# Half of an MLP's first quarter turned from row-block products into seven block products

## The chip, the core and the metric

The kernel runs on one core of a Trainium2 chip. Its time is the device time of one execution, in microseconds; of several runs the median counts. The core has five engines with queues of their own: PE (TensorE, matmuls; PEld are its weight loads), DVE (VectorE), ACT (ScalarE), POOL (GpSimd, here mostly issuing transfers that add to what is in SBUF) and SP (issuing plain transfers). An engine starts its instructions in the order of its queue.

## The reference, cut to what matters

A two-layer encoder over 512 tokens of width 1024: attention and an MLP, then a recurrent block and an MLP, then a norm. The change is in the second MLP.

```python
def squared_relu_mlp(h, w1, w2):
    u = jax.nn.relu(h @ w1)          # 1024 -> 4096
    return (u * u) @ w2              # 4096 -> 1024
...
    h = rms_norm(x, norm_mlp[layer])
    x = x + squared_relu_mlp(h, mlp_w1[layer], mlp_w2[layer])
```

## The kernel before, in words

**Arithmetic.** Every fp32 product is made of three matmuls: both operands are split into a rounded high part (by ACT, a CAST or a scaled ACTIVATE) and a low part, operand minus high (by DVE), and high x high, high x low and low x high are added in PSUM. A weight tile so costs ACT one 1024-wide cast (`wh`) and DVE one 1024-wide subtraction (`wl`). The norm's factor per token is left out of x (only its gain g goes in: `xgh`, `xgl`) and multiplied into the MLP's result (`rr`).

**x.** x lies transposed, as eight tiles of 128 features x 512 tokens. `residual` (L767) adds the output projection to each tile and makes `xgh` and `xgl`. `Squares` adds up the squares of x over the tiles; four small matmuls (L172) sum them over the features.

**The MLP.** The 4096 hidden features are taken in four quarters; each has an upward product (x to hidden) and a downward one (hidden to the result). A quarter is two halves p = 0, 1 of 512 hidden features.

The downward products of all quarters and the upward products of the quarters 1 to 3 are done by the Strassen-Winograd scheme: the operands are cut into 2 x 2 blocks, and seven block products, P1 to P7 (`PRODUCTS`), replace eight. Blocks of weights are added with each other before (`added`: P5's and P6's sums on DVE, P7's and P4's by adding transfers that POOL issues), and so are blocks of x (`sums_of_x`, four additions on DVE for each of four pairs k of x tiles: tile k and tile 4 + k) with high and low parts of their own (`halves_of_sums`: `s41`, `s2`, `s3` and the `low` tiles). A block product is 24 matmuls of 256 columns (`up`, L991). Products add up in PSUM banks named X, V and W: P1, P6, P7 and P4 go to X, P5 and P3 to V, P2 to W, and between products what stands in a bank is copied to or combined with the slots u[0] to u[3] of the half (`leave`, L1249): `keep` says which results ACT copies out, the table behind it which DVE adds to a slot. Each slot then gets relu and square (ACT), and a high and a low part.

The first quarter is different. Its upward product is made row block by row block: eight chunks of 128 hidden features, each 24 matmuls of 512 columns (`squared`, L863; `quarters`, L1356). The first two run side by side (`beside`), since the last x tile comes late. Each chunk's result gets relu and square on ACT; two chunks make a pair for which DVE forms sums (`split`, `sums`). Beside the chunks 1 to 4, `between` (L1658) turns x, with 32 transposes on PE and eight copies on ACT, into the tiles c in which the result is collected. The sums of x for the pairs 0 and 1 are made behind chunks 4 and 5, those for pairs 2 and 3 during the first downward quarter, at set places (`leave`, places 19 to 26), since the block products need them only for the second quarter.

**What sets the order.** PE's order is the program's. In the MLP, ACT and DVE run through `Ordered`, which makes each instruction be issued behind the one written before it. `run` walks a list of steps; for step i it loads what is due at its place, handles what step i - 1 left (`leave`), prepares the weights of a later step (`prepare`, `make`: high and low part, about four steps ahead) and issues step i's matmuls. P1 comes first in a half, then P5, P6, P3, P7, P2, P4 (`UP`).

Of the kernel before, what the change touches and what calls it, by code (L numbers as in the profile page):

```python
# [64 lines left out]
def hybrid_encoder(  # L65
# [41 lines left out]
    def f(ap):  # L107
        return ap.bitcast(F32)
# [107 lines left out]

    def slab(src, cut=1, ks=range(C), at=0):
        raws = rawpools[next(loads) % len(rawpools)]
        raw = raws.tile([P, C, P], F32, tag="raw", name="raw", bufs=3 if raws is wpool else 1)
        k = slice(ks.start, ks.stop)  # L220
        nc.sync.dma_start(out=raw[:, k, :], in_=src[:, k, :])
        pool = wpools[next(slabs) % len(wpools)]
        wh = half_slab(pool, "wh", at)
        wl = half_slab(pool, "wl", at)
        for i in range(cut):
            k = slice(ks.start + i * len(ks) // cut, ks.start + (i + 1) * len(ks) // cut)
            A.copy(wh[:, k, :], raw[:, k, :])  # L227
            with tc.issue_after(behind[0]) if behind[0] else nullcontext():
                V.tensor_tensor(wl[:, k, :], raw[:, k, :], f(wh[:, k, :]), ALU.subtract)  # L229
        return wh, wl  # L230
# [535 lines left out]

    def residual(srcs, gname, begun={}, ready={}):  # L767

        for c in range(C):
            add_x(c, begun[c][0] if c in begun else dense(srcs[c], bh, bl, halves=ready.get(c)))  # L770
            halves(gname, c, x[c])

    residual(w_so, "mlp0", so, so_next)


# [23 lines left out]
    class Mlp:  # L799
# [27 lines left out]

        def __init__(self, ctx, layer):
            self.layer, self.sq, self.first = layer, Squares(), None
# [33 lines left out]
        def squared(self, c):  # L863

            if self.first is None:

                self.first = [bank("z") if self.layer else self.bank() for _ in range(2)]
                self.turns = count(2)
                ws = [slab(w_m1[self.layer, i]) for i in range(2)]
                beside(ws, xgh, xgl, self.first, {})  # L870
            if self.first:
                ps = self.first.pop(0)
            else:
                ps = dense(w_m1[self.layer, c], xgh, xgl, ps=self.bank())
            p, i, a = c // 4, c % 4 // 2, c % 2
# [95 lines left out]
        def replace(self):  # L971

            for i, t in enumerate(self.s3):
                self.A.copy(xgh[:, 2 * i : 2 * i + 2, HS:], f(t).rearrange("p (k n) -> p k n", k=2))

        def slots_of(self, p):

# [54 lines left out]
        def from_up(self, q4):  # L1032
            return self.units(
                [
                    lambda tag, p=p: w_up[self.layer, q4 - 1, p, *self.SOURCES[tag]].rearrange(
                        "p k n -> p (k n)"
# [104 lines left out]
        OPEN_AT = 36  # L1141
        UP = "P1", "P5", "P6", "P3", "P7", "P2", "P4"
        STEPS = 28

        def run(self, first, between, end):
# [4 lines left out]

            steps = []
            for q4 in range(NQ):
# [4 lines left out]
            units, ws, sums, us = {("down", 0): first}, {}, {}, {}  # L1157

            def place(i):

                return (i + self.STEPS // 2) % self.STEPS

# [57 lines left out]
            def load(i):  # L1220
                q4, at = steps[i][1], place(i)

                if i == 0:
                    self.turns = count(2)
                elif at == 0:
# [16 lines left out]
            def prepare_or_hold(i, then=None):  # L1242

                if i + 1 < len(steps) and steps[i + 1][0] == "up" and steps[i + 1][3] == "P1":
                    held.append(i + 4)
# [3 lines left out]
            def leave(i):  # L1249
# [5 lines left out]
                if kind == "down":  # L1255
                    ahead = q4 == 0 and place(i) == 25
                    if ahead:
# [4 lines left out]
                    if not ahead:  # L1262
                        prepare_or_hold(i)
                    if q4 == 0:

# [55 lines left out]
            waiting, later, held = [], [], []  # L1321
            make(0)
            add(1)
            make(1)
            add(5, 4)
            for e in (self.V, self.A):
                e.turn(True)
            self.squared(C - 1)
            self.split(1, 1, slice(0, 3), slice(0, 3))
            make(2)  # L1330
            self.sums(1, 1)
            add(4, 2)
            make(3)
            self.split(1, 1, slice(0, 4), slice(3, 7))
            between(C - 1)
            for i, (kind, q4, g, name) in enumerate(steps):
# [7 lines left out]
                if name == "P1":  # L1344
                    us[g] = self.slots_of(g)
# [6 lines left out]
            for e in (self.V, self.A):  # L1352
                e.turn(False)
            end([ws[len(steps) - 2 + g] for g in range(2)], sums["down", NQ - 1, 0]["X"])

        def quarters(self, between, end):  # L1356
# [292 lines left out]

    residual(w_ro, "mlp1", begun, {4: ws["o4"]})  # L1650
    wctx.close()


    with ExitStack() as mctx:
        lp = mctx.enter_context(tc.tile_pool(name="last", bufs=1))
        mlp = Mlp(mctx, 1)

        def between(c):  # L1658

            t = c - 1  # L1660
            if t not in range(NB):
                return
            for h in range(2):
                pt = mlp.bank()
                for i in range(4):
                    PE.transpose(
                        pt[:, i * P : (i + 1) * P], x[4 * h + i][:, t * P : (t + 1) * P], ident
                    )
                A.copy(mlp.y(t, h), pt)
                mlp.begun.add((t // 2 * 2 + h, t % 2))  # L1670
# [106 lines left out]
        end.ready = factors  # L1777
        mlp.quarters(between, end)

# [68 lines left out]
```

## Time and profile before

| | |
|---|---|
| runs | 1029.29, 1029.65, 1030.36 us; median 1029.65 |
| span of the profiled execution, first to last instruction | 1027.3 us (its own time is not recorded apart) |
| PE busy | 1018.6 us, 99% |
| DVE, ACT, POOL busy | 857.7, 701.1, 173.1 us |
| first upward quarter of the last MLP | 703.02 to 751.13, 48.11 us |
| downward quarter behind it | 751.13 to 789.66, 38.53 us |

A row of a timeline gives an instruction's start, its duration, engine, line, operation, what it writes from what it reads, and in brackets the idle time ahead of it with what ended it. Records overlap a little, so two neighbours' starts tell more of the pace than one duration. Tiles are named by the program: `ps_z`, `ps_o`, `ps_acc`, `ps_t` are PSUM banks (two of each), b weight blocks, u hidden values, s, `bh`, `bl`, `sh`, `sl` high and low parts. Most of the MLP's ACT and DVE work is recorded by one helper line (L789).

### The profile page before, as it was taken

The numbers are of one execution on the slowest core, as the hardware profiler recorded it, in microseconds if no ns is written. First come the engines' busy times: TensorE is split into PE (matmuls) and PEld (weight loads), VectorE is DVE, ScalarE is ACT, GpSimd is POOL, SyncE is SP. The second block draws the span as 40 slices with busy tenths as digits, with TensorE's granted clock in tenths as the row PEclk, the third lists the DMA queues.
The fourth block names the chain that finished last, engine by engine and source line by source line (L and its number), as shares of the span: only waits on it lengthen the run. The fifth ranks groups of instructions, "written<-read, shape, count | busy, mean of one in ns | idle before, by whom it ended". The sixth has DMA issues, their size and how long they took to land.

```text
span 1027.3 us, 15935 instructions
## 1 busy us (share of the span) xinstructions
PE 1018.6 (99%) x5890; PEld 892.4 (87%) x5890; DVE 857.7 (83%) x1150; ACT 701.1 (68%) x1084; POOL 173.1 (17%) x239
## 2 busy tenths in 40 slices
PE   9999999999999999999999999999999999999997
PEld 8988888888888988988988888888888988988986
DVE  7988787848788898898899888984689898898897
ACT  7777676826766773873875799964755773863866
POOL 0454443420010010010011121200010010010012
PEclk9999999999999999999999999999999999999999
DMA  7745453528537667667682675452436677667653
GB/s 241 225 112 147 126 147 99 166 87 298 141 67 202 174 146 200 173 142 205 180 203 78 160 184 148 103 208 99 97 72 182 175 154 196 172 145 203 171 115 108
DMA packets 53260, 160.46 MB, mean 156 GB/s; under 512 B 6720, under 2 KB 8256, under 8 KB 53184
## 3 DMA queue, kind: packets, MB, share of 16 engines
q1 hardware_dynamic: 42240, 120.48, 35.6%
q0 software_dynamic: 10656, 38.80, 22.7%
q8 instruction: 46, 0.75, 0.3%
q14 instruction: 30, 0.25, 0.1%
q10 hardware_dynamic: 288, 0.18, 0.1%
HBM read 137.41 MB, written 4.19 MB: 138 GB/s over the span
## 4 chain that ended last, share of the span: by engine, by line
PE 95%; ACT 2%; DVE 2%; issue 1%; ACTq 0%; DVEq 0%
PE ps_t L1135 16%; PE ps_acc L1000 9%; PE ps_acc L1135 9%; PE ps_z L1000 7%; PE ps_acc L236 5%; PE ps_acc L234 5%; PE ps_acc L235 5%; PE ps_z L1135 4%; PE ps_o L1000 4%; PE ps_t L234 2%; PE ps_t L236 2%; PE ps_t L235 2%; PE ps_o L234 2%; PE ps_o L236 2%; PE ps_o L235 2%; PE ps_t L628 2%
## 5 line engine op out<-in xcount | busy, mean ns | idle before, releaser
L789 ACT CAST wh<-b 128x1024 fp32r<-128x1024 f32 x168 | 173.9, 1050 | 116.0 <-DVE b L789 73.1
L789 DVE TENSOR_TENSOR wl<-b,wh 128x1024 fp32r<-128x1024 f32 x168 | 203.1, 1221 | 37.6 <-ACT wh L789 36.4
L1076 POOL DMA_DIRECT2D b<-in_w_dn x40 | 35.0, 876 | 364.2 <-DVE b L789 268.4
L234 PE MATMUL ps_acc<-xgh,wh 128*128 128x512 f32 x192 | 78.5, 409 | 0.0
L236 PE MATMUL ps_acc<-xgl,wh 128*128 128x512 f32 x192 | 75.2, 392 | 0.0
L235 PE MATMUL ps_acc<-xgh,wl 128*128 128x512 f32 x192 | 75.1, 391 | 0.0
L229 DVE TENSOR_TENSOR wl<-raw,wh 128x512 fp32r<-128x512 f32 (+2 forms) x70 | 62.2, 915 | 15.1 <-ACT wh L227 15.0
L789 ACT ACTIVATE u<-u 128x512 f32<-128x512 f32 x100 | 63.2, 633 | 14.2 <-DVE u L789 12.6
L606 DVE TENSOR_TENSOR_SCAN scan<-keep,later 128x128 f32<-128x128 f32 (+1 forms) x64 | 58.3, 914 | 16.3 <-POOL w L600 8.1
L227 ACT CAST wh<-raw 128x512 fp32r<-128x512 f32 (+2 forms) x70 | 50.7, 759 | 21.1 <-PE ps_acc L236 7.3
L610 POOL TENSOR_TENSOR w<-w,scan 128x128 f32<-128x128 f32 (+1 forms) x64 | 52.8, 827 | 55.4 <-DVE scan L606 50.8
L1076 POOL DMA_DIRECT2D b<-in_w_up x24 | 20.9, 870 | 231.0 <-DVE b L789 64.8
L789 DVE TENSOR_TENSOR b<-b,b 128x1024 f32<-128x1024 f32 x48 | 58.7, 1223 | 1.2
L789 DVE TENSOR_TENSOR u<-u 128x512 f32<-128x512 f32 (+1 forms) x92 | 54.9, 597 | 4.5 <-ACT u L789 2.5
L789 ACT CAST wh<-raw 128x1024 fp32r<-128x1024 f32 x46 | 48.1, 1048 | 2.5 <-PE ps_acc L1135 2.4
L1135 PE MATMUL ps_t<-wh,bh 128*128 128x512 f32 x120 | 47.0, 392 | 0.1
L1135 PE MATMUL ps_t<-wh,bl 128*128 128x512 f32 x120 | 46.8, 390 | 0.0
L789 DVE TENSOR_TENSOR sl<-u,sh 128x512 fp32r<-128x512 f32 (+2 forms) x50 | 37.5, 750 | 10.3 <-ACT sh L789 10.3
L1000 PE MATMUL ps_z<-xgh,wh 128*128 128x256 f32 x192 | 45.0, 277 | 0.2
L789 DVE TENSOR_TENSOR wl<-raw,wh 128x1024 fp32r<-128x1024 f32 x36 | 44.3, 1231 | 0.8 <-ACT wh L789 0.8
L1000 PE MATMUL ps_acc<-low,wh 128*128 128x256 f32 x192 | 44.7, 276 | 0.0
L789 DVE TENSOR_TENSOR bl<-u,bh 128x1024 fp32r<-128x1024 f32 (+2 forms) x26 | 33.9, 1304 | 12.4 <-ACT bh L789 12.3
(419 smaller groups left out, 3219.8 us busy)
## 6 DMA issues: line engine op xcount, KB each, us to landing
b<-in_w_dn SPq DMA_DIRECT2D x48, 512.0 KB, 4.4
b<-in_w_dn POOLq DMA_DIRECT2D x40, 512.0 KB, 5.8
b<-in_w_up SPq DMA_DIRECT2D x36, 512.0 KB, 4.8
b<-in_w_up POOLq DMA_DIRECT2D x24, 512.0 KB, 5.6
raw<-in_w_m SPq DMA_DIRECT2D x16, 512.0 KB, 3.9
raw<-in_w_dn SPq DMA_DIRECT2D x16, 512.0 KB, 4.5
raw<-in_w_in SPq DMA_DIRECT2D x16, 512.0 KB, 3.8
raw<-in_w_qk SPq DMA_DIRECT2D x12, 512.0 KB, 3.9
```

The costliest lines, as they stand in the source:

```text
L227: A.copy(wh[:, k, :], raw[:, k, :])
L229: V.tensor_tensor(wl[:, k, :], raw[:, k, :], f(wh[:, k, :]), ALU.subtract)
L234: PE.matmul(ps, wh, ah, start=start, stop=False)
L235: PE.matmul(ps, wl, ah, start=False, stop=False)
L236: PE.matmul(ps, wh, al, start=False, stop=stop)
L606: V.tensor_tensor_scan(sc[:, S - n : S][:, ::-1], keep[:, :n][:, ::-1], later[:, S - n :][:, ::-1], 1.0, ALU.mult, ALU.max,)
L610: G.tensor_tensor(wt, wt, sc[:, S - n + 1 : S + 1], ALU.mult)
L628: PE.transpose(tr[:, (qb - kb) * P : (qb - kb + 1) * P], w[pair, j, qb][:, kb * P : (kb + 1) * P], ident,)
L789: ins = getattr(self.e, name)(*args, **kwargs)
L1000: PE.matmul(ps[:, i * HS : (i + 1) * HS], m, y, start=new and i == k == low == 0 and y is h, stop=(low, i, k) == steps[-1], skip_group_che ...
L1076: G.dma_start(out=unit[b].rearrange("p j n -> p (j n)"), in_=unit["src"](to), accum_op=ALU.add)
L1135: PE.matmul(sums[to][i], a[:, j, block, i * P : (i + 1) * P], y[:, j, :], start=new and g == j == n == 0 and a is h, stop=g == j == 1 and ...
```

## The change

Only the last MLP changes. The first half (p = 0) of its first quarter stays four chunks. Its second half (p = 1) becomes seven block products, as in the later quarters. For that:

- All 32 transposes of x come first: 16 ahead of the stage's first chunk matmul, 16 behind the first six (`between(0)`, `between(1)`), since the sums of x are formed in place.
- The sums of x, now scaled by the gain within the additions (`scaled_sums_of_x`), and their high and low parts are made at the head, for all four pairs, and no longer in the downward quarter.
- The order of the opening half is P2, P1, P5, P6, P3, P7, P4 (`OPENING`). P2 needs no sum of x. So ACT copies P2 out, and DVE adds P1 to it out of P1's bank.
- Weights: three blocks of `w_up` for the half and three of `w_dn` are loaded ahead of the stage; `w_up` now holds all four quarters. The squares of x are asked for in `residual`.

```diff
+        OPENING = "P2", "P1", "P5", "P6", "P3", "P7", "P4"
...
+        def scaled_sums_of_x(self, k):
+            lo, hi = slice(0, HS), slice(HS, S)
+            u, v = x[k], x[C // 2 + k]
+            gu, gv, minus = self.gains(k)
+            add = self.V.scalar_tensor_tensor
+            add(v[:, hi], u[:, hi], gu, v[:, hi], ALU.mult, ALU.subtract)
+            self.V.tensor_tensor(u[:, hi], u[:, lo], u[:, hi], ALU.subtract)
+            add(u[:, lo], u[:, lo], minus, v[:, hi], ALU.mult, ALU.add)
+            add(v[:, lo], v[:, lo], gv, u[:, lo], ALU.mult, ALU.add)
...
-                keep = {"P1": 0, "P6": 1, "P5": 2, "P7": 3}.get(name)
+                keep = {"P1": 0, "P6": 1, "P5": 2, "P7": 3}
+                if i < opening:
+                    keep["P2"] = keep.pop("P1")
+                keep = keep.get(name)
...
-                    "P2": (0, u[0], three, ALU.add),
+                    "P1" if i < opening else "P2": (0, u[0], three, ALU.add),
...
+            def mixed_lead():
+                ws = [slab(w_m1[self.layer, c], e=(self.A, self.V)) for c in (2, 3)]
+                for e in (self.V, self.A):
+                    e.turn(True)
+                between(0)
+                beside(self.ws, xgh, xgl, self.first, {1: lambda: between(1)})
+                for k in range(4):
+                    self.scale_of_x(k)
+                self.scaled_sums_of_x(0)
+                self.highs_of_sums(0)
+                self.scaled_sums_of_x(1)
+                self.highs_of_sums(1)
+                self.lows_of_sums(0)
+                self.scaled_sums_of_x(2)
+                for c in range(2):
+                    self.hidden(c, self.first[c])
+                self.split(0, 0, slice(0, 3), slice(0, 3))
+                make(0)
+                self.highs_of_sums(2)
+                self.lows_of_sums(1)
+                make(1)
+                add(2)
+                ps = dense(None, xgh, xgl, halves=ws[0], tag="t")
+                self.rr = self.sq.inv_squares(bank("t"))
+                self.scaled_sums_of_x(3)
+                self.hidden(2, ps)
+                self.highs_of_sums(3)
+                make(2)
+                self.lows_of_sums(2)
+                self.lows_of_sums(3)
+                self.sums(0, 0)
+                ps = dense(None, xgh, xgl, halves=ws[1], tag="acc")
+                self.hidden(3, ps)
+                self.split(0, 1, slice(0, 3), slice(0, 3))
+                add(3)
+                make(3)
+                self.place_s3()
+                self.sums(0, 1)
```

How the engines' rows move, at three places. A row is a line of the kernel, an operation, what it writes from what it reads, and its size; xN stands for N equal rows in a row, and in brackets stand the engines whose semaphores it waits for. The helper line L789 of before is L791 after, `up` is L1056 instead of L1000.

PE, at the head of the stage. Before, the last residual chunk (`ps_o<-bl`) is followed by the chunks 0 and 1, with transposes only behind them:

```order
L236 MATMUL ps_o<-bl,wh 128x512
L234 MATMUL ps_z<-xgh,wh 128x512
L235 MATMUL ps_z<-xgh,wl 128x512
L236 MATMUL ps_z<-xgl,wh 128x512
...
L1666 MATMUL ps_t<-ident,x 128x128 x8
```

After, the transposes stand between, and the fifth waits for DVE:

```order
L236 MATMUL ps_o<-bl,wh 128x512
L1795 MATMUL ps_o<-ident,x 128x128 x4
L1795 MATMUL ps_o<-ident,x 128x128 [waits DVE_49]
L1795 MATMUL ps_o<-ident,x 128x128 x3
L1795 MATMUL ps_t<-ident,x 128x128 x8
L234 MATMUL ps_z<-xgh,wh 128x512 [waits Activation_49]
```

The first four transposes write the free bank of the pair `ps_o`, the next four the one that the residual product has just left.

PE, in the second half. Before, chunk matmuls follow each other, here the last of chunk 6, the column sums of the squares and the start of chunk 7:

```order
L236 MATMUL ps_z<-xgl,wh 128x512
L172 MATMUL ps_z<-ones,ssq 128x1 [waits Activation_49]
L172 MATMUL ps_z<-ones,ssq 128x1 x3
L234 MATMUL ps_o<-xgh,wh 128x512 [waits PE_49,Activation_49]
L235 MATMUL ps_o<-xgh,wl 128x512 [waits DVE_49]
```

After, two pieces: the end of P5 with the start of P6, and the end of P7 with the start of P4:

```order
L1056 MATMUL ps_o<-s_7414,wl 128x256 x8
L1056 MATMUL ps_o<-bh,wh 128x256 [waits DVE_49,Activation_49]
L1056 MATMUL ps_o<-low,wh 128x256
...
L1056 MATMUL ps_o<-xgh,wl 128x256 x7
L1056 MATMUL ps_o<-xgh,wh 128x256 [waits Activation_49]
L1056 MATMUL ps_o<-xgl,wh 128x256
```

P6 (moving operand `bh`) now waits for DVE before its first matmul, and P4 for ACT.

DVE, beside the last chunks. Before, low parts of the last hidden values (`sl`) and of the downward weights (`wl`) take turns:

```order
L789 TENSOR_TENSOR sl<-u,sh 128x1024
L789 TENSOR_TENSOR sl<-u,sh 128x768
L789 TENSOR_TENSOR wl<-b_7465,wh 128x1024
L789 TENSOR_TENSOR u<-u 128x256 x4
L789 TENSOR_TENSOR b_7465<-b_7465,b_7467 128x1024
L789 TENSOR_TENSOR wl<-raw,wh 128x1024
```

After, this is what stands from P5's weights up to the addition of P1 (`u<-u,ps_o`):

```order
L791 TENSOR_TENSOR wl<-b_7435,wh 128x1024
L791 TENSOR_TENSOR low<-x,s_7414 128x512
L791 TENSOR_TENSOR low<-x,bl 128x256
L791 SCALAR_TENSOR_TENSOR low<-x,colt,sh 128x256
...
L791 TENSOR_TENSOR u<-u 128x256 x4
L791 TENSOR_TENSOR bl<-u,bh 128x768
L791 TENSOR_TENSOR b_7435<-b_7435,b_7439 128x1024
L791 TENSOR_TENSOR wl<-b_7435,wh 128x1024
L791 TENSOR_TENSOR u<-u 128x256 x4
L791 TENSOR_TENSOR wl<-b_7439,wh 128x1024
L791 TENSOR_TENSOR u<-u,ps_o 128x512
```

The addition of P1 stands behind the low parts of the last two pairs of x's sums, the sums and low part of the chunks, and the weights of P6 and P3.

More of the change, by code (lines that the diff above doesn't have):

```diff
@@ L765, in add_x, with residual @@
         V.tensor_tensor(x[c], x[c], ps, ALU.add)
[L767 removed]
+    def residual(srcs, gname, begun={}, ready={}, squares=None):
         for c in range(C):
@@ L771, in residual @@
             halves(gname, c, x[c])
+            if squares:
+                squares.chunk(c, x[c])
     residual(w_so, "mlp0", so, so_next)
@@ L826, in hybrid_encoder, with __init__ @@
         BANKS = "oottaazz"
-        def __init__(self, ctx, layer):
-            self.layer, self.sq, self.first = layer, Squares(), None
+        def __init__(self, ctx, layer, squares=None):
+            self.layer, self.sq, self.first = layer, squares or Squares(), None
+            self.mixed = squares is not None
             self.V, self.A = Ordered(V), Ordered(A)
@@ L1151, in run @@
             steps = []
+            if self.mixed:
+                steps += [("up", 0, 1, name) for name in self.OPENING]
+            opening = len(steps)
             for q4 in range(NQ):
@@ L1223, in load @@
                 if i == 0:
-                    self.turns = count(2)
+                    self.turns = count(7 if opening else 2)
                 elif at == 0:
@@ L1255, in leave @@
                 if kind == "down":
-                    ahead = q4 == 0 and place(i) == 25
+                    begin = q4 == 0 and not opening
+                    ahead = begin and place(i) == 25
                     if ahead:
@@ L1321, in run, with lead @@
             waiting, later, held = [], [], []
[L1322 to L1335, printed above, removed]
+            def lead():
+                make(0)
+                add(1)
+                make(1)
+                add(5, 4)
+                for e in (self.V, self.A):
+                    e.turn(True)
+                self.squared(C - 1)
+                self.split(1, 1, slice(0, 3), slice(0, 3))
+                make(2)
+                self.sums(1, 1)
+                add(4, 2)
+                make(3)
+                self.split(1, 1, slice(0, 4), slice(3, 7))
+                between(C - 1)
@@ L1343, in run @@
                     continue
-                if name == "P1":
+                if (kind, q4, g) not in sums:
                     us[g] = self.slots_of(g)
@@ L1354, in run, with mixed_quarters @@
             end([ws[len(steps) - 2 + g] for g in range(2)], sums["down", NQ - 1, 0]["X"])
+        def mixed_quarters(self, between, end):
+            self.minus = small.tile([P, C], F32, tag="minus", name="minus")
+            V.tensor_scalar(self.minus, col(f"mlp{self.layer}"), -1.0, None, ALU.mult)
+            self.first = [bank("z") for _ in range(2)]
+            self.ws = [slab(w_m1[self.layer, c]) for c in range(2)]
+            tags = [(p, b) for p in range(2) for b in ("b11", "b12", "b22")]
+            self.slots = {at: i for i, at in enumerate(tags)}
+            ups = [
+                {"src": lambda tag, p=p: w_up[self.layer, 0, p, *self.SOURCES[tag]].rearrange(
+                    "p k n -> p (k n)"
+                )}
+                for p in range(2)
+            ]
+            self.load(ups, *tags[3:])
+            downs = self.from_down(0)
+            self.load(downs, (0, "b11"), (0, "b12"), (1, "b11"))
+            self.run((ups, downs), between, end)
+            self.blocks.close()
         def quarters(self, between, end):
@@ L1655, in hybrid_encoder, with between @@
         lp = mctx.enter_context(tc.tile_pool(name="last", bufs=1))
[L1656 to L1664, printed above, removed]
+        mlp = Mlp(mctx, 1, last_squares)
+        def between(h):
+            for t, tag in enumerate((("o", "o", "t", "t"), ("acc", "acc", "o", "o"))[h]):
+                pt = bank(tag)
                 for i in range(4):
@@ L1777, in hybrid_encoder @@
         end.ready = factors
-        mlp.quarters(between, end)
+        mlp.mixed_quarters(between, end)
 COLS = {}
```

71 lines of the change are left out of this document (59 added, 12 removed).

## The prediction

> **What bounds the kernel now.** I read the page's busy shares and its chain, then two stretches, then the timelines of PE, DVE and ACT in them.
>
> ```profile
> span 1027.3 us, 15935 instructions
> ...
> PE 1018.6 (99%) x5890; PEld 892.4 (87%) x5890; DVE 857.7 (83%) x1150; ACT 701.1 (68%) x1084; POOL 173.1 (17%) x239
> ...
> PE 95%; ACT 2%; DVE 2%; issue 1%; ACTq 0%; DVEq 0%
> ```
>
> PE is the bound: 99% busy, 95% of the chain. A PE microsecond saved is a microsecond, as long as its operands come in time. The span is 1027.3, the runs' median 1029.65; the 2.35 outside the span I leave as they are and add the stage's change to the median.
>
> The changed stage is the last MLP's first upward quarter, 703.02 to 751.13; the downward quarter behind it ends at 789.66 (columns: stretch, its length, then busy us and count of PE, PEld, DVE, ACT, POOL).
>
> ```profile
> 703.02:751.13 48.11, 48.11 (x233) 40.25 (x232) 28.76 (x46) 29.49 (x47) 1.76 (x2) 1.00 0.32 77
> 751.13:789.66 38.53, 38.46 (x169) 31.38 (x168) 34.30 (x45) 21.88 (x28) 3.46 (x4) 1.00 0.57 152
> ```
>
> PE fills the stage, and DVE has 28.8 us of work in 48.1. Prices on PE, from its timeline:
>
> ```profile
> 703.02 0.39 PE L234 MATMUL ps_z<-xgh,wh 128*128 128x512 f32 x1
> ...
> 713.90 1.03 PE L1666 MATMUL ps_t<-ident,x 128*128 128x128 f32 x8
> 714.69 0.48 PE L234 MATMUL ps_acc<-xgh,wh 128*128 128x512 f32 x1
> 715.01 0.40 PE L235 MATMUL ps_acc<-xgh,wl 128*128 128x512 f32 x1
> ...
> 744.74 0.95 PE L172 MATMUL ps_z<-ones,ssq 128*128 128x1 f32 x8
> 745.55 0.49 PE L234 MATMUL ps_o<-xgh,wh 128*128 128x512 f32 x1
> ```
>
> ```profile
> 800.72 0.28 PE L1000 MATMUL ps_acc<-xgh,wh 128*128 128x256 f32 x1
> ...
> 803.44 0.28 PE L1000 MATMUL ps_z<-xgh,wh 128*128 128x256 f32 x1
> ```
>
> The time of one record overlaps its neighbours, so I take start to start. 48 wide matmuls from 703.02 to 713.90: 0.2267 each, 5.44 a chunk of 24. A block product of 24 narrow ones, 800.72 to 803.44: 2.72. Eight transposes: 0.79, and 0.09 more in the matmul behind (0.32 instead of 0.23): 0.88. The column sums: 0.81 and 0.1: 0.9.
>
> **The change, part by part.** Zero is the end of the product before the stage.
>
> *The products.* Four chunks (4 x 5.44 = 21.76) become seven block products (7 x 2.72 = 19.04): -2.72, all on PE, so all on the path.
>
> *The transposes* are as many, but now come first. The second group needs the PSUM bank of the last residual product, and so its addition on DVE:
>
> ```profile
> 703.22 0.69 DVE L765 TENSOR_TENSOR x<-x,ps_o 128x512 f32<-128x512 f32 x1 [1.86 <-PE ps_o L236]
> ```
>
> It ends 703.91, 0.89 after zero; the first group of four is through at 0.4. PE waits 0.5. Chunks 0 and 1 are done at 2 x 5.44 + 4 x 0.88 + 0.5 = 14.9, chunks 2 and 3 at 14.9 + 5.44 + 0.9 + 5.44 = 26.7; P2, P1, P5 end at 34.8, where P6 would start. P2 needs no sum of x, and so hides some of their work.
>
> *Who waits.* P6 adds into the bank that P1 filled. In the later quarters ACT copies P1 out first; here DVE adds P1 to the kept P2 (P2 and P1 are swapped), and that addition stands behind everything that DVE was given earlier. So its queue decides P6. It starts anew when ACT has made relu, square and high half of chunks 0 and 1. Prices:
>
> ```profile
> 751.33 0.60 ACT L789 ACTIVATE u<-ps_o 128x512 f32<-128x512 f32 x1 [1.40 <-PE ps_o L236]
> 751.96 0.63 ACT L789 ACTIVATE u<-u 128x512 f32<-128x512 f32 x1
> 752.62 0.84 ACT L789 CAST sh<-u 128x768 fp32r<-128x768 f32 x1
> ```
>
> ```profile
> 753.50 0.96 DVE L789 TENSOR_TENSOR sl<-u,sh 128x768 fp32r<-128x768 f32 x1 [2.31 <-ACT sh L789]
> 754.44 1.23 DVE L789 TENSOR_TENSOR wl<-b,wh 128x1024 fp32r<-128x1024 f32 x1
> 755.59 1.79 DVE L789 TENSOR_TENSOR u<-u 128x256 f32<-128x256 f32 x4
> 757.30 1.22 DVE L789 TENSOR_TENSOR b<-b,b 128x1024 f32<-128x1024 f32 x1
> 758.43 1.22 DVE L789 TENSOR_TENSOR wl<-raw,wh 128x1024 fp32r<-128x1024 f32 x1
> ...
> 777.02 0.42 DVE L789 TENSOR_TENSOR low<-x,bl 128x256 fp32r<-128x256 f32 x1
> 777.35 1.22 DVE L789 TENSOR_TENSOR low<-x,s 128x256 fp32r<-128x256 f32 x2
> 778.49 1.22 DVE L789 TENSOR_TENSOR wl<-raw,wh 128x1024 fp32r<-128x1024 f32 x1
> ```
>
> ```profile
> L511 DVE SCALAR_TENSOR_TENSOR v<-ps_acc,rc,v 128x256 fp32r<-128x256 f32 x14 | 6.7, 476 | 2.1 <-ACT v L510 2.0
> L789 DVE TENSOR_TENSOR x<-x 128x256 f32<-128x256 f32 x32 | 13.5, 423 | 2.7 <-ACT x L789 2.3
> ```
>
> From PE to DVE there it takes 753.50 - 751.33 = 2.2. Here 0.2 for the last matmul to drain and 0.5 for the other chunk's relu and square come on top: DVE starts at 14.9 + 2.9 = 17.8. In the order after the change it then has, start to start: two 768-wide halves (0.94 each, 1.9); low halves of the weights of P2, P1, P5, P6, P3 (5 x 1.14 = 5.7); two block sums of weights (2 x 1.13 = 2.3); low halves of x's sums for pairs 1, 2, 3 (777.02 to 778.49: 3 x 1.47 = 4.4); pair 3's sums (four at 0.43, 1.7); two times four sums of u (1.71 each, 3.4); three tiny ones of the norm (0.3); the addition of P1 (0.7). Six of the narrow ones now take a scalar as well: 476 against 423 ns, 0.3 in all. That is 20.7 us of work.
>
> In between DVE stands still twice, for ACT. P5's low half needs its high half, which ACT makes behind the three casts of pair 3's sums; P6's needs a cast of the block sum that DVE has just made:
>
> ```profile
> 788.35 0.41 ACT L789 CAST bl<-x 128x256 fp32r<-128x256 f32 x1 [0.18 <-DVE x L789]
> 788.66 0.92 ACT L789 CAST s<-x 128x256 fp32r<-128x256 f32 x2
> ...
> 808.92 1.05 ACT L789 CAST wh<-b 128x1024 fp32r<-128x1024 f32 x1 [1.60 <-DVE b L789]
> ```
>
> 788.35 to 789.58 and 1.05: 2.3; the second 1.05 and two handovers: 1.2. Sum 17.8 + 20.7 + 2.3 + 1.2 = 42.0. P6 starts there and not at 34.8: **7.2 us of idle PE**.
>
> *Behind it.* ACT's pace, copies and wide casts by turns:
>
> ```profile
> 794.55 0.57 ACT L789 COPY u<-ps_acc 128x512 f32<-128x512 f32 x1
> 795.02 1.04 ACT L789 CAST wh<-b 128x1024 fp32r<-128x1024 f32 x1
> 795.97 0.58 ACT L789 COPY u<-ps_acc 128x512 f32<-128x512 f32 x1
> ```
>
> Behind P1's addition it makes relu, square and cast of the new block (0.63 + 0.66 + 0.5), copies P5 (0.5), and takes three 1024-wide casts (0.95 each) before it copies P6 (0.6): 5.7, while P6 and P3 take 5.44, so P7 waits 0.3. P4 adds into P7's bank directly after P7 (in the later quarters P2 stands between). ACT copies P7 behind a cast for which DVE must first do five 1024-wide steps, and these start with P7's high half, 3.3 after P6's start: 3.3 + 5.7 + 1.05 + 0.6 = 10.7. P7 ends at 5.75 + 2.72 = 8.5: P4 waits 2.2. P4 ends 42.0 + 10.7 + 2.7 = 55.4.
>
> *What is hidden.* The copies of the transposes and the sums of pairs 0 to 2 lie on ACT and DVE beside chunks 0 and 1; DVE is through with them before 17.8. The squares of x have moved only in the text: both orders have them beside the residual. Three blocks of w_up are loaded on SP ahead of the stage and P2's raw block in it, P7's and P4's sums go through POOL:
>
> ```profile
> b<-in_w_up SPq DMA_DIRECT2D x36, 512.0 KB, 4.8
> b<-in_w_up POOLq DMA_DIRECT2D x24, 512.0 KB, 5.6
> ```
>
> P4's sum is issued behind P6's low half, some 3.6 before P6 starts, and lands 2.0 after; ACT wants it 3.3 + 0.95 after. If it came 3 later, P7 and P4 would wait that long.
>
> *Given back.* The downward quarter loses pairs 2 and 3 of the sums on DVE. Of its stalls this one could go:
>
> ```profile
> 782.96 1.07 PE L1135 MATMUL ps_z<-wl,sh 128*128 128x512 f32 x4
> 784.10 0.47 PE L1135 MATMUL ps_t<-wh,bh 128*128 128x512 f32 x1
> ```
>
> 1.14 where four wide matmuls take 0.91: -0.2.
>
> **The sum.** The stage takes 55.4 instead of 48.1, +7.3; less 0.2 is +7.1. 1029.65 + 7.1 = **1036.7**.
>
> **Rivals.**
>
> *The clock falls in the gap.* At the program's start PE is slow:
>
> ```profile
> core 0: 1027.3 us, clock 0.998
> ...
> 1.13 4.66 PE L396 MATMUL ps_z<-dense_ones 128*128 128x128 bf16 x42 [1.13 <-DVE dense_ones L118]
> 5.55 1.10 PE L433 MATMUL ps_acc<-xgh,wh 128*128 128x512 f32 x2
> ```
>
> 42 matmuls of 128 columns take 4.42 to the next one's start, 105 ns each, where the wide ones take 57 per 128 columns; half speed for 4.4 us is 0.002 of the span, just what 0.998 lacks. Nowhere does before let PE idle for microseconds later on. If the gap at P6 brings the slow clock back for as long, 2.2 us of product time are lost. ACT and DVE do not wait for it up to P7, so the 0.3 and part of the 2.2 ahead of P4 swallow some: 0.4 to 2.2 more, 1037.1 to 1038.9, say **1038.3**. Chance 0.19. [...]
>
> *Less waiting.* The two waits for ACT (3.5) vanish behind other work: P6 waits 3.7 and P4 about 1, the stage takes 50.7, +2.6 less 0.2: **1032**. Chance 0.11.
>
> *Balance.* DVE needs 5 us less than summed: no change, 1029.65. Chance 0.03.
>
> *DVE is early* (faster). If P1's addition is done at 35, no product waits: -2.72 + 0.5 - 0.2, **1027.2**. It decides at P6's first matmul; the work alone, without waits, reaches 38.5, so the rows speak against it. The same time would follow if P6 did not wait for the addition, but the order has its wait for DVE at that very row. The sum of some forty steps is where I can be most wrong, so chance 0.10.
>
> **The numbers.** The forecast has 0.57, its own range 1035 to 1038.2 (one us for the sum of some forty steps on DVE either way). With the clock's case and less waiting (half a us to its own sides) the range is 1031.5 to 1039.0; it leaves out balance and early DVE, 0.13. Within 0.2% (2 us, about what a measurement of this kernel tells from no change) 0.03, faster 0.10, slower 0.87.
>
> **What would show it.** Right: in the after profile PE idles about 7 us ahead of the fourth block product (bh as its moving operand), released by DVE's addition into u, and about 2 ahead of the seventh, released by ACT's copy; the seven take 2.72 each, chunks 2 and 3 run without gaps; 168 narrow matmuls replace 96 wide ones. Wrong: P6 follows P5 without a gap, or its wait ends with weights or a DMA; narrow matmuls slower than 0.1133; the loss in the downward quarter.

## The result, and the profile after

The changed kernel takes 1036.95 us (median of 5 runs, 1036.29 to 1037.63) against 1029.65: 1.0070 times as long, 95% interval 1.0059 to 1.0081. The forecast was 1036.7.

The head of the profile after, the shares of its chain, and the waits of PE between 700 and 805 us (columns: who waited in what for whom, us in total, times, the longest):

```profile
span 1035.1 us, 16103 instructions
...
PE 1017.7 (98%) x5962; PEld 894.5 (86%) x5962; DVE 866.0 (84%) x1158; ACT 705.4 (68%) x1089; POOL 174.5 (17%) x241
...
PE 90%; DVE 5%; ACT 3%; DMA 1%; issue 1%; POOL 0%; ACTq 0%; DVEq 0%
```

```profile
PE ps_o L1056 <- DVE u L791: 6.6, 1, 6.6
PE ps_o L1056 <- ACT u L791: 1.1, 1, 1.1
PE ps_o L1795 <- DVE x L765: 0.3, 1, 0.3
```

The span is 7.8 longer. PE is busy 0.9 less, although one product ran at half speed for 2.95 us of its time (P6, granted clock 0.50, below), so the products did become cheaper. What is new are three waits: the prediction had put waits in these three places and a small one, ahead of P7, in a fourth. DVE, which had 2% of the chain, now has 5%.

The stage and the downward quarter behind it, in the view by stretches (columns as before the change):

```profile
703.58:759.35 55.77, 47.77 (x305) 43.26 (x304) 41.01 (x64) 37.35 (x60) 3.49 (x4) 0.94 0.33 80
759.35:797.46 38.11, 38.11 (x171) 31.54 (x169) 34.56 (x39) 19.16 (x24) 3.45 (x4) 1.00 0.74 178
```

The stage takes 55.77 instead of 48.11 (+7.66), the quarter behind it 38.11 instead of 38.53 (-0.42). The stage begins 0.56 later than before: PE's rows lag by 0.24 from 5.8 us on and by 0.58 from 210 us on, long ahead of the stage, and why was not traced. 7.66 - 0.42 + 0.56 = 7.8, the whole difference of the spans; nothing is lost elsewhere.

PE's timeline, its first rows at the head and the starts of the products:

```profile
703.58 0.60 PE L1795 MATMUL ps_o<-ident,x 128*128 128x128 f32 x4
704.52 0.66 PE L1795 MATMUL ps_o<-ident,x 128*128 128x128 f32 x4 [0.34 <-DVE x L765]
...
730.40 0.28 PE L1056 MATMUL ps_z<-xgh,wh 128*128 128x256 f32 x1
...
736.06 0.28 PE L1056 MATMUL ps_o<-s,wh 128*128 128x256 f32 x1
...
737.94 1.10 PE L1056 MATMUL ps_o<-s,wl 128*128 128x256 f32 x8
745.65 0.55 PE L1056 MATMUL ps_o<-bh,wh 128*128 128x256 f32 x1 [6.60 <-DVE u L791]
746.00 0.41 PE L1056 MATMUL ps_o<-low,wh 128*128 128x256 f32 x1
746.21 0.41 PE L1056 MATMUL ps_o<-bh,wh 128*128 128x256 f32 x1
...
749.85 0.28 PE L1056 MATMUL ps_o<-s,wh 128*128 128x256 f32 x1
...
752.57 0.28 PE L1056 MATMUL ps_o<-xgh,wh 128*128 128x256 f32 x1
...
756.51 0.39 PE L1056 MATMUL ps_o<-xgh,wh 128*128 128x256 f32 x1 [1.06 <-ACT u L791]
...
759.35 0.40 PE L1191 MATMUL ps_t<-wh,bh 128*128 128x512 f32 x1
```

Zero is 703.58. The row at 745.65 is P6: it starts at 42.07, and DVE's addition into u releases it. P5 ends at about 738.9 by the pace of its starts, so PE stands for 6.8 us (the 6.60 in the row counts from the end of P5's last record, which overlaps). P4, at 756.51 (52.93), waits for ACT. P6 itself takes 4.20 (to 749.85) where P3 and P7 take 2.72.

DVE's timeline shows why P6 is late: where this engine stood still, and the addition.

```profile
721.40 0.96 DVE L791 TENSOR_TENSOR bl<-u,bh 128x768 fp32r<-128x768 f32 x1 [3.69 <-ACT bh L791]
...
731.73 1.23 DVE L791 TENSOR_TENSOR wl<-b,wh 128x1024 fp32r<-128x1024 f32 x1 [2.34 <-ACT wh L791]
...
740.83 1.23 DVE L791 TENSOR_TENSOR wl<-b,wh 128x1024 fp32r<-128x1024 f32 x1 [1.11 <-ACT wh L791]
...
744.82 0.68 DVE L791 TENSOR_TENSOR u<-u,ps_o 128x512 f32<-128x512 f32 x1
```

It starts anew at 17.82, stands twice for ACT (2.34 and 1.11), and comes to the addition of P1 at 744.82. P1's matmuls had ended where P5's begin, at 736.06.

### The profile page after: what moved, and what is told of

It reads as the page before. It is cut to its first block, busy times and chain, and to the rows that moved or that the text cites. A ratio compares the mean times of both kernels' runs of the same rounds, so it can differ in the third digit from the quotient of the medians.

```text
span 1035.1 us, 16103 instructions
## 1 busy us (share of the span) xinstructions
PE 1017.7 (98%) x5962; PEld 894.5 (86%) x5962; DVE 866.0 (84%) x1158; ACT 705.4 (68%) x1089; POOL 174.5 (17%) x241
## 4 chain that ended last, share of the span: by engine, by line
PE 90%; DVE 5%; ACT 3%; DMA 1%; issue 1%; POOL 0%; ACTq 0%; DVEq 0%
PE ps_t L1191 16%; PE ps_acc L1056 9%; PE ps_acc L1191 8%; PE ps_z L1056 7%; PE ps_o L1056 4%; PE ps_acc L236 4%; PE ps_acc L234 4%; PE ps_acc L235 4%; PE ps_z L1191 4%; PE ps_t L234 2%; PE ps_t L235 2%; PE ps_t L236 2%; PE ps_o L234 2%; PE ps_o L236 2%; PE ps_o L235 2%; PE ps_t L628 1%
## 5 line engine op out<-in xcount | busy, mean ns | idle before, releaser
L791 ACT CAST wh<-b 128x1024 fp32r<-128x1024 f32 x174 | 180.3, 1050 | 126.1 <-DVE b L791 83.9
L791 DVE TENSOR_TENSOR wl<-b,wh 128x1024 fp32r<-128x1024 f32 x174 | 210.5, 1220 | 42.3 <-ACT wh L791 40.8
L791 ACT ACTIVATE u<-u 128x512 f32<-128x512 f32 x103 | 65.0, 632 | 17.1 <-DVE u L791 15.1
L234 PE MATMUL ps_acc<-xgh,wh 128*128 128x512 f32 x184 | 75.3, 409 | 0.0
L236 PE MATMUL ps_acc<-xgl,wh 128*128 128x512 f32 x184 | 72.1, 392 | 0.0
L235 PE MATMUL ps_acc<-xgh,wl 128*128 128x512 f32 x184 | 72.0, 391 | 0.0
L791 DVE TENSOR_TENSOR b<-b,b 128x1024 f32<-128x1024 f32 x50 | 61.2, 1223 | 1.3
L791 DVE TENSOR_TENSOR u<-u 128x512 f32<-128x512 f32 (+1 forms) x89 | 55.0, 617 | 4.5 <-ACT u L791 2.5
L229 DVE TENSOR_TENSOR wl<-raw,wh 128x512 fp32r<-128x512 f32 (+2 forms) x64 | 54.2, 876 | 5.3 <-ACT wh L227 5.3
L791 ACT CAST wh<-raw 128x1024 fp32r<-128x1024 f32 x49 | 51.2, 1048 | 10.1 <-PE ps_acc L1191 4.0
L227 ACT CAST wh<-raw 128x512 fp32r<-128x512 f32 (+2 forms) x64 | 44.4, 732 | 16.0 <-PE ps_acc L236 7.3
L791 DVE TENSOR_TENSOR wl<-raw,wh 128x1024 fp32r<-128x1024 f32 x39 | 48.0, 1230 | 1.6 <-ACT wh L791 1.6
L1056 PE MATMUL ps_z<-xgh,wh 128*128 128x256 f32 x200 | 46.9, 277 | 0.2
L791 DVE TENSOR_TENSOR sl<-u,sh 128x512 fp32r<-128x512 f32 (+2 forms) x53 | 37.9, 716 | 9.1 <-ACT sh L791 9.1
L791 DVE TENSOR_TENSOR bl<-u,bh 128x1024 fp32r<-128x1024 f32 (+2 forms) x26 | 33.9, 1304 | 13.8 <-ACT bh L791 13.7
L1056 PE MATMUL ps_acc<-low,wh 128*128 128x256 f32 x192 | 44.7, 276 | 0.0
```

The lines of the kernel that those rows point to most:

```text
L227: e[0].copy(wh[:, k, :], raw[:, k, :])
L229: e[1].tensor_tensor(wl[:, k, :], raw[:, k, :], f(wh[:, k, :]), ALU.subtract)
L234: PE.matmul(ps, wh, ah, start=start, stop=False)
L235: PE.matmul(ps, wl, ah, start=False, stop=False)
L236: PE.matmul(ps, wh, al, start=False, stop=stop)
L791: ins = getattr(self.e, name)(*args, **kwargs)
```

## The experiments

Two theories were to be told apart. **A**: from the end of the chunks on, the half runs at the pace of the queues of DVE and ACT; P6 is only the first place where PE meets them. **B**: the loss is one dependence, P6's wait for that addition. Beside them stood **C**, that the clock, which fell in the gap, costs something of its own. The runs of before that stood beside these eight had medians of 1029.90 (e1 to e4) and 1029.73 (e5 to e8). In the table, P6, P4 and the stage's end are us from zero, the start of the stage's first transpose, in the profiled execution of each run.

| | median, us | ratio to before, interval | P6 | P4 | end |
|---|---|---|---|---|---|
| the change | 1036.95 | 1.0070 (1.0059 to 1.0081) | 42.07 | 52.93 | 55.77 |
| e1 P1 copied by ACT | 1037.26 | 1.0074 (1.0061 to 1.0086) | 38.60 | 52.83 | 55.68 |
| e2 sums early on DVE | 1033.10 | 1.0034 (1.0022 to 1.0045) | 37.47 | 48.33 | 51.26 |
| e3 one wait filled | 1038.19 | 1.0083 (1.0070 to 1.0096) | 42.06 | 52.92 | 57.14 |
| e4 other order, one part left out | 1029.78 | 0.9999 (0.9990 to 1.0009) | 33.72 | 45.03 | 47.86 |
| e5 other order | 1031.44 | 1.0015 (1.0006 to 1.0024) | 34.91 | 45.79 | 48.51 |
| e6 more on DVE | 1039.79 | 1.0096 (1.0083 to 1.0110) | 44.12 | 55.66 | 58.50 |
| e7 both waits filled | 1037.37 | 1.0077 (1.0063 to 1.0091) | 42.07 | 52.93 | 55.78 |
| e8 waits removed | 1027.23 | 0.9978 (0.9969 to 0.9988) | 31.93 | 43.24 | 46.06 |

**e1.** The dependence alone is taken away.

```diff
-        OPENING = "P2", "P1", "P5", "P6", "P3", "P7", "P4"
+        OPENING = "P1", "P2", "P5", "P6", "P3", "P7", "P4"
...
-                if i < opening:
-                    keep["P2"] = keep.pop("P1")
...
-                    "P1" if i < opening else "P2": (0, u[0], three, ALU.add),
+                    "P2": (0, u[0], three, ALU.add),
```

> Order P1, P2, P5, P6, P3, P7, P4; ACT copies P1 out of its bank and DVE adds P2, which no product waits for. The new wait of P6 is so for ACT's copy and for its own weights, no longer for DVE's addition. Theory A (behind P5 the half runs at the pace of DVE's and ACT's queues, and P6 is only the first place where PE meets them): P6 starts at about 742.3 (its low weights end at 742.06 and the copy at 742.23 in the profile after), 3.4 earlier; then P3 waits about 3 us for ACT's copy of P5 (ends 747.96), P7 about 0.6 for that of P6 (ends 751.29), and P4 starts where it did, 756.5: the time stays 1036.9, within 0.6. Theory B (the addition in P6's path alone is the loss): what P6 gains is kept, 1036.95 - 3.4 = 1033.6.

The median is 1037.26 us. PE's timeline in e1, the rows that wait (P6, P3, P7, P4), and ACT's copy of P7, which P4 waits for, first in e1 and then in the change:

```profile
741.79 0.58 PE L1056 MATMUL ps_z<-bh,wh 128*128 128x256 f32 x1 [3.11 <-ACT u L791]
...
747.53 0.39 PE L1056 MATMUL ps_o<-s,wh 128*128 128x256 f32 x1 [1.34 <-ACT u L791]
...
750.86 0.39 PE L1056 MATMUL ps_z<-xgh,wh 128*128 128x256 f32 x1 [0.33 <-ACT u L791]
...
756.02 0.39 PE L1056 MATMUL ps_z<-xgh,wh 128*128 128x256 f32 x1 [2.07 <-ACT u L791]
```

```profile
755.39 0.58 ACT L791 COPY u<-ps_z 128x512 f32<-128x512 f32 x1
```

```profile
755.88 0.58 ACT L791 COPY u<-ps_o 128x512 f32<-128x512 f32 x1
```

P6 starts 3.5 earlier, no longer behind DVE, and the gain is gone by P4: the two waits ahead of P6 and P4 have become four, all for ACT. The copy that P4 waits for starts 52.20 from zero in e1 and 52.30 in the change, so moving P6 did not move the queues. A's 1036.9, within 0.6, holds, and B, which had 1033.6, falls. The largest wait alone would have misled here, since it halved; that P4 starts where it did (52.83 against 52.93) is what tells. The clock was at half in e1 too (0.51 from 741.44 to 744.85), so P6 was slow there as well (0.21 a matmul, 742.17 to 742.38); the waits behind it show that PE had caught up with ACT again all the same.

**e2.** The same work on DVE and ACT in another order, with the products as in the change.

```diff
                 self.scaled_sums_of_x(2)
+                self.lows_of_sums(1)
+                self.highs_of_sums(2)
+                self.scaled_sums_of_x(3)
+                self.lows_of_sums(2)
                 for c in range(2):
                     self.hidden(c, self.first[c])
                 self.split(0, 0, slice(0, 3), slice(0, 3))
                 make(0)
-                self.highs_of_sums(2)
-                self.lows_of_sums(1)
                 make(1)
+                self.highs_of_sums(3)
                 add(2)
+                make(2)
+                self.lows_of_sums(3)
                 ps = dense(None, xgh, xgl, halves=ws[0], tag="t")
                 self.rr = self.sq.inv_squares(bank("t"))
-                self.scaled_sums_of_x(3)
                 self.hidden(2, ps)
-                self.highs_of_sums(3)
-                make(2)
-                self.lows_of_sums(2)
-                self.lows_of_sums(3)
                 self.sums(0, 0)
```

> Only the order on DVE and ACT changes: the low parts of the sums of x for the pairs 1 and 2 and pair 3's sums are written ahead of relu of the chunks 0 and 1, into DVE's wait of 3.69 us that ends at 721.40, and pair 3's casts behind the high parts of P2 and P1. Nothing is left out. Theory A (DVE's queue decides): 1.47 + 1.47 + 1.72 = 4.7 us of DVE's work leave the stretch from 17.8 us to the addition of P1, so P6 starts about 4.7 earlier, its wait falls from 6.8 to about 2, and the time to 1032.2 (1031.5 to 1033.5). Rival (the path runs over ACT and the weights of P6 and P3, and DVE's low parts only fill waits): P6's wait loses less than 2 us, 1035 or more.

The median is 1033.10 us. PE's timeline in e2, P6 and P4:

```profile
741.72 0.36 PE L1056 MATMUL ps_o<-bh,wh 128*128 128x256 f32 x1 [2.00 <-DVE u L791]
...
752.58 0.39 PE L1056 MATMUL ps_o<-xgh,wh 128*128 128x256 f32 x1 [2.15 <-ACT u L791]
```

P6 and P4 both start 4.6 earlier than in the change, and the stage is 4.5 shorter: what leaves DVE's queue ahead of the addition comes off the stage at its full length, as A had it (4.7). The median gains 3.85, inside the expected range; in the profiled execution the stage begins 0.67 later than in the change, which makes up the rest.

**e6.** The opposite: work is added there.

```diff
+                spare = work.tile([P, S], F32, tag="sq", name="spare")
+                V.memset(spare, 0.0)
...
                 make(3)
+                for n in range(3):
+                    self.V.tensor_tensor(spare, spare, spare, ALU.add)
                 self.place_s3()
```

> The change as made, with three additions of 512 columns on a spare tile in DVE's queue ahead of P3's low weights' sums and so ahead of the addition of P1: 3 x 0.62 = 1.9 us (55.0 us for 89 in the profile's groups), whose result nobody reads. Theory A (each us in DVE's queue ahead of that addition is a us of the kernel): P6 starts 1.8 later, 1038.8, within 0.6, or up to 1.4 more where the half speed falls on P4. Rival (DVE has slack there, P6 is released by something else): 1037.

The median is 1039.79 us, 2.8 more than the change and 0.4 above the 1039.4 that A allowed without half speed in P4. The added group on DVE, then P6 and P4 on PE:

```profile
742.35 2.14 DVE L791 TENSOR_TENSOR spare<-spare 128x512 f32<-128x512 f32 x3
```

```profile
748.08 0.55 PE L1056 MATMUL ps_o<-bh,wh 128*128 128x256 f32 x1 [8.65 <-DVE u L791]
...
759.62 0.38 PE L1056 MATMUL ps_o<-xgh,wh 128*128 128x256 f32 x1 [0.68 <-ACT u L791]
```

The three additions take 2.06 to the next one's start (742.35 to 744.41), and P6 starts 2.05 later (44.12). A holds from both sides: a microsecond on DVE is a microsecond at P6. P4 starts another 0.7 later; that arises behind P6, which here ran at half speed all through (0.50 up to 753.3) and took 5.25 instead of 4.20. P4 itself ran at full speed (2.84).

**e3.** Spare matmuls keep PE busy in P6's wait; their bank is not read.

```diff
+                if i == 3:
+                    fill = bank("z")
+                    for n in range(28):
+                        PE.matmul(fill, xgh[:, 4, :P], xgh[:, 4, :], start=n == 0, stop=n == 27)
                 self.up(name, ws.pop(i), banks[to], new)
```

> 28 matmuls of 512 columns into a spare bank, never read, stand between P5 and P6 and keep PE busy for 6.35 us of its wait. Both theories expect full speed in P6 (2.72 instead of 4.20). Theory A (the half speed is covered by the waits behind it): P3 ends 1.4 earlier, P7 waits about 0.3 for ACT's copy of P6, P4 waits 2.4 instead of 1.2, and the time stays 1036.9, within 0.4. Theory C (the clock's fall costs what P6 lost): 1036.95 - 1.4 = 1035.5.

The median is 1038.19 us, which neither had; the profiled execution took 1039.48. First the clock in the change itself, by stretches (the column behind POOL's is the granted clock), then PE's timeline in e3 from P6 on, and the clock there:

```profile
738.87:741.75 2.88, 0.17 (x2) 0.00 (x0) 1.77 (x2) 2.00 (x3) 0.00 (x0) 1.00 0.00 0
741.75:748.60 6.85, 2.95 (x14) 2.98 (x15) 4.34 (x8) 4.42 (x7) 0.86 (x1) 0.50 0.66 148
748.60:756.51 7.91, 6.85 (x61) 6.66 (x60) 7.54 (x8) 6.12 (x8) 0.86 (x1) 1.00 0.42 140
```

```profile
739.75 6.54 PE L1466 MATMUL ps_z<-xgh 128*128 128x512 f32 x28
746.51 0.36 PE L1056 MATMUL ps_o<-bh,wh 128*128 128x256 f32 x1 [0.23 <-DVE u L791]
...
757.37 0.38 PE L1056 MATMUL ps_o<-xgh,wh 128*128 128x256 f32 x1 [2.16 <-ACT u L791]
...
758.82 0.42 PE L1056 MATMUL ps_o<-xgl,wh 128*128 128x256 f32 x1
759.03 0.41 PE L1056 MATMUL ps_o<-xgh,wh 128*128 128x256 f32 x1
...
761.59 0.61 PE L1191 MATMUL ps_t<-wh,bh 128*128 128x512 f32 x1
```

```profile
755.20:758.58 3.38, 1.22 (x11) 1.21 (x11) 3.38 (x5) 2.61 (x4) 0.86 (x1) 1.00 0.40 85
758.58:762.00 3.42, 3.42 (x17) 3.34 (x17) 2.85 (x4) 3.33 (x6) 0.87 (x1) 0.51 1.03 180
```

In the change the clock was at half (0.50) from 741.75 to 748.60, and P6's matmuls took 0.21 each there (746.00 to 746.21). In e3 P6 ran at full speed (0.12 a matmul, 746.70 to 746.82), and P4 started 10.86 behind P6's start in both (757.37 - 746.51 and 756.51 - 745.65): what P6 had lost was wholly covered by the wait ahead of P4, 1.06 there and 2.16 here. So far A holds, and C does not. But that longer wait let the clock fall in P4 instead (0.51 from 758.58 to 762.00, matmuls 0.21 apart at 758.82 to 759.03), and behind P4 no wait covers it: P4 takes 4.22 instead of 2.84.

**e7** puts that to the test: e3's 28 spare matmuls and nine more in the wait ahead of P4.

```diff
...
+                if i == 6:
+                    fill = bank("z")
+                    for n in range(9):
+                        PE.matmul(fill, xgh[:, 4, :P], xgh[:, 4, :], start=n == 0, stop=n == 8)
```

> As e3, with nine more spare matmuls (2.04 us) in the wait ahead of P4 that e3 showed (2.16). Theory A with the clock (e3's P4 ran at half speed from 1.25 us after its start, since PE had stood idle for 2.1 us of the stretch before, and no wait behind P4 covers that): no half speed at all, P4 starts where it did, 52.9 after zero, and takes 2.8: the stage 55.8 and the time 1036.9, within 0.5, that is 1.3 less than e3. Rival (the half speed in P4 came from keeping PE busy, not from its idle time): 1038.2 or more.

The median is 1037.37 us. PE's timeline in e7, the second filling, P4 and the downward quarter, and the clock over the half:

```profile
754.57 2.23 PE L1470 MATMUL ps_z<-xgh 128*128 128x512 f32 x9
756.80 0.38 PE L1056 MATMUL ps_o<-xgh,wh 128*128 128x256 f32 x1
...
759.65 0.40 PE L1191 MATMUL ps_t<-wh,bh 128*128 128x512 f32 x1
```

```profile
736.00:760.00 24.00, 23.76 (x164) 21.56 (x163) 19.35 (x26) 15.58 (x21) 2.59 (x3) 1.00 0.50 122
```

The clock stays whole (1.00), P4 takes 2.85, and the stage takes what it took in the change, 55.78, though PE rested in only 0.24 of these 24 us. So a clock kept whole gains nothing over the change, and C falls. The traces settle this; the medians alone do not: the intervals of e3 and e7 overlap, and two of e3's five runs seem to have had no fall in P4 (mean clock 0.998 and 0.999, 1036.91 and 1037.71 us, against 1038.19 to 1040.21 at 0.997).

**e4** and **e5** take the order of the later quarters, P1, P5, P6, P3, P7, P2, P4, with P1 copied by ACT as in e1. In e4 the block sum of P5's weights was left out, because the calls that add blocks went by places in the old order; e5 puts the sum back.

```diff
-        OPENING = "P2", "P1", "P5", "P6", "P3", "P7", "P4"
+        OPENING = "P1", "P5", "P6", "P3", "P7", "P2", "P4"
...
                 make(0)
+                add(1)
...
                 make(1)
                 add(2)
...
-                add(3)
                 make(3)
```

(The lines `add(1)` and `add(3)` differ in e5 alone; e4 kept them as in the change.)

> The half in the order of the later quarters, P1, P5, P6, P3, P7, P2, P4, with ACT copying P1 and DVE adding P2 late. P2's 2.7 us lie between P7 and P4, and P2's weights and the block sum of P6 come at other places in DVE's queue. Theory A: P5 waits about 1.3 for its low parts, since it comes a product earlier; P6, P3 and P7 are served by then, and P4 hardly waits: of the 8 us of waits in this half about 1.5 are left, 1029.6 (1028.5 to 1031.5). Theory B (the addition in P6's path alone): 1033.6, since P4's wait stays in some form. If the moved work at the head is itself too much for DVE in any order: 1035 or more.

> The order of the later quarters once more; e4 had left one part out, the addition of b12 to b11 ahead of P5's weights (1.22 us on DVE, 1.13 start to start), which is back here. Nothing is left out. Theory A (DVE's queue decides): the addition stands ahead of all that P5 waits for, so P5's wait of 1.0 in e4 becomes about 2.2, nothing else waits, and the time is 1029.8 + 1.2 = 1031.0 (1030.2 to 1032), still some 6 below the change as made. Rival (e4 was fast because P5 had nothing to wait for, and P6's wait comes back once P5's weights are right): 1034 or more.

The medians are 1029.78 us (e4) and 1031.44 us (e5). PE's timeline in e5: all that waits in the half, the start of the downward quarter and that of the product behind it:

```profile
735.72 0.39 PE L1056 MATMUL ps_o<-low,wh 128*128 128x256 f32 x1 [0.90 <-DVE low L791]
...
737.30 0.38 PE L1056 MATMUL ps_o<-low,wh 128*128 128x256 f32 x1 [1.07 <-DVE low L791]
...
752.93 0.40 PE L1191 MATMUL ps_t<-wh,bh 128*128 128x512 f32 x1
...
792.21 0.28 PE L1056 MATMUL ps_acc<-xgh,wh 128*128 128x256 f32 x1
```

Of 7.7 us of waits among the products 2.0 are left, both in P5 for the low parts of x's sums; P6 (34.91) follows P5 without one, and so does every product behind it. Between e4 and e5 P6 moved by 1.19, as expected, but the median by 1.7: e5's stage ends 0.65 later, and its downward quarter takes 39.28 where e4 has 38.68 and the change 38.11. DVE is busy for 37.20 us of that quarter in e5 and for 34.56 in the change, which suggests that DVE work left over from the half holds it up; this was not tested. The order, with P1 copied by ACT (worth nothing by itself, as e1 showed), is worth 5.5 of the 7.3 that the change lost.

**e8** joins e2 and e5, with small steps of its own: the first transposes go to banks that are free, the move of s3 into xgh stands behind ACT's copy of P1, and the weights of P1 and pair 3's high and low parts come a little earlier in the order. Two of these:

```diff
-            for t, tag in enumerate((("o", "o", "t", "t"), ("acc", "acc", "o", "o"))[h]):
+            for t, tag in enumerate((("t", "t", "o", "o"), ("acc", "acc", "o", "o"))[h]):
...
+                if i == 2 and opening:
+                    self.place_s3()
```

> All together, nothing left out: the order P1, P5, P6, P3, P7, P2, P4 with P1 copied by ACT; the sums of pair 3 and the low parts of the pairs 1 and 2 ahead of relu of the chunks 0 and 1; the first transposes into the free bank pair ps_t instead of ps_o; xgh overwritten behind the copy of P1. Theory A: no wait of PE over 0.3 us is left in the stage: chunks and transposes end 26.3 after zero, seven products at 2.83 (as they took in e2 and e4) are 19.8, together 46.1, 2.0 less than the stage before, and 0.4 less in the downward quarter as after the change: 1029.9 - 2.4 = 1027.5 (1026.5 to 1029). Rival (the moved work does not fit beside four chunks in any order, or takes itself back in the downward quarter): 1029.5 or more.

The median is 1027.23 us, 0.9978 of before (0.9969 to 0.9988): faster than before by 2.5 and than the change by 9.7, and inside the expected range. PE's row at the first product, and the stage and its downward quarter by stretches:

```profile
729.50 0.28 PE L1056 MATMUL ps_z<-xgh,wh 128*128 128x256 f32 x1
```

```profile
703.23:749.29 46.06, 46.06 (x305) 42.13 (x304) 39.69 (x62) 36.16 (x59) 2.61 (x3) 1.00 0.36 90
749.29:787.40 38.11, 38.11 (x171) 31.54 (x169) 35.67 (x41) 20.00 (x25) 4.33 (x5) 1.00 0.77 186
```

PE is busy for all of the 46.06. So the block products do pay, by 2.05 in the stage, once DVE's work is in the order in which PE needs it.

## Why the prediction was right, step by step

- *The products cost 2.72 less.* Near it. They were priced at 2.72 each from a later quarter; here P2 and P1 took 2.83 each (730.40 to 736.06), as did all seven of e8 (19.79 in all), so the saving is 21.76 - 19.8 = 2.0. That is 0.118 a matmul, so a sign that the prediction had named as wrong, narrow matmuls slower than 0.1133, did come. In the change the extra hid in P6's wait.
- *The head: 0.5.* Right: the second transposes start 0.94 behind zero, 0.89 was given. The chunks end at 14.99 and 26.82, given were 14.9 and 26.7.
- *DVE starts at 17.8, stands 2.3 and 1.2, and P6 starts at 42.0.* Right: 17.82, 2.34, 1.11, 42.07. The wait is 6.8 and not 7.2 because the products ahead end at 35.3 and not at 34.8. e2 and e6 show that it hangs on the length of that queue, one to one.
- *P7 waits 0.3, P4 waits 2.2, P4 ends at 55.4.* The end is near (55.77); the waits came out as none and 1.2, because P6 lost 1.5 to the clock. With full speed in P6, in e3, P4 waits 2.16, and P7 still does not wait: P6 and P3 take 5.73 there and not 5.44.
- *P4's wait, priced from P6's start.* The prediction let the wait for ACT's copy of P7 follow from P6's start. e1 moved P6 and P4 stayed, so both hang on DVE's and ACT's queues side by side. This did not alter the sum, and it is why the sum came out: PE's own products took 20.97 in the change instead of 19.04, and its waits 8.0 instead of 9.7, since the queues set where P6 and P4 start.
- *The clock rival, 0.19.* The fall came about and its price did not. The forecast's own case had the clock stay up; that was wrong, and that its number survived was luck in this one point: the rival was given 0.4 to 2.2 in net price, P6 lost 1.5, and the wait ahead of P4 covered all of it. PE stood from 738.9, and the granted clock was 0.50 from 741.75, after 2.9 us, to 748.60: 6.85 us, where the rival had taken 4.4 from the program's start. The prediction also misread before's clock: what 0.998 lacks lies at the program's end and not at its start, and so before did hold a row for the fall (last section).
- *Less waiting, balance, early DVE.* None came: DVE's two waits for ACT (2.34 and 1.11) are there in full, and DVE is not ahead of its sum.
- *Given back, 0.2.* It was 0.42: PE is busy for all of the quarter's 38.11 us. But this hangs on what DVE still has to do when the quarter begins: e5's quarter has no sums of x to make either, and yet takes 39.28, more than before.

## What to carry to other kernels

An engine that is 83% busy over the whole kernel can be the bound of one stage: there, list its queue in program order up to the instruction that the bottleneck waits for, and add it up from the time at which it can start. When one wait is taken away, look at where a later product starts, not at the wait: only if that moves has the path become shorter. Work that is moved to an earlier stage should be issued into the gaps that its engine has there, and products that need the least prepared should stand where the others' operands are made. In this kernel that was P2 between P7 and P4.

## What the runs showed of the hardware

The granted clock was at half (0.50 or 0.51) for 6.85 us in the change, 3.42 in e3 and 10.2 in e6. In the change it fell 2.9 us after PE had come to rest. In e3 it fell 1.2 us after PE had resumed, behind a wait of 2.16; PE had worked for 1.22 of the 3.38 us ahead of the fall. In e2's profiled execution two waits of 2.0 and 2.15 did not bring it down: it was 1.00 over 20 us that hold both, of which PE worked for 15.84. Why it fell behind 2.16 and not behind 2.15, these runs do not show. The row of e2, then the slow stretch of e6, then the end of before:

```profile
736.00:756.00 20.00, 15.84 (x131) 15.37 (x130) 15.67 (x19) 15.64 (x21) 2.59 (x3) 1.00 0.56 134
```

```profile
743.10:753.30 10.20, 5.22 (x24) 5.25 (x25) 7.32 (x11) 5.65 (x8) 0.60 (x1) 0.50 0.50 104
```

```profile
1023.60:1027.30 3.70, 0.00 (x0) 0.00 (x0) 0.00 (x0) 0.00 (x0) 0.00 (x0) 0.50 0.39 142
```

In before no matmul runs from 1020.4 on, and the last 3.7 us are at half (0.50): that is 0.0018 of the span, what the mean clock of 0.998 lacks. The slow matmuls at its start (105 ns each) are not in that mean, for which the view has 1.00 there.

In e6 PE stood for the first 5.0 us of the slow stretch (743.1 to 748.08) and worked for the rest; from 753.3 on the clock was 1.00. Up to its rise PE had worked at half speed for 2.95 us in the change, 3.42 in e3 and 5.22 in e6, so the rise did not follow one fixed amount of work; each was read from one execution only.

The same 24 narrow matmuls took 2.83 us (0.118 each) in some stretches and 2.72 (0.113) in others, at a granted clock of 1.00 in both: 2.83 for all seven of e8, 2.72 in e5 from P6 on and for P3 and P7 of the change. What makes the difference was not tried.
